# A two-layer decoder trunk: cross-attention's V projection moved to the start, half of K into layer 0's gated attention, layer 0's residual brought forward, FFN output parts of 8, 6 and 8 tiles

## The chip, the cores and the metric

The kernel runs on one core of one Trainium2 chip. The metric is the device time of one launch in microseconds (us). The kernel before was run three times: 1430.82, 1432.17 and 1435.38 us, median 1432.17. One further execution was profiled. All durations below come from that profile.

Engines are named as in the profile: PE is the matrix engine (PEld its weight loads), DVE the vector engine, ACT the activation engine, POOL the third elementwise engine, SP the engine that issues most DMA transfers. A name with q (SPq, PEq) is the engine's instruction queue.

## The reference

The input x is 512 tokens of 1024 numbers in fp32, `mem` is 256 memory tokens of 1024. After one layer norm come two layers, each of three sub-layers with `x <- LayerNorm(alpha*x + f(x))`:

```
proj = h @ w_in                          # columns: c_a 512, c_g 512, q 256, k 256, v 512, r 512, a_low 16
u  = silu(layer_norm(causal_conv31(c_a * sigmoid(c_g))))          # 31 taps per channel
o  = rms_norm(gla_chunked(q, k, v, log_a)) * silu(r)              # 4 heads, chunks of 64 tokens
h  = LN(alpha*h + concat(u, o) @ w_mix_out)
kv = mem @ w_xkv;  K, V = split(kv)                               # does not depend on h
h  = LN(alpha*h + softmax((h@w_xq) K^T / 16) V @ w_xo)            # 4 heads of 256
g, u = split(h @ w_ffn_in);  h = LN(alpha*h + (silu(g)*u) @ w_ffn_out)   # hidden width 2816
```

K and V of a layer need only `mem` and that layer's `w_xkv`, so they may be computed at any time before that layer's cross-attention.

## The kernel before, in words

Activations stay on chip, as four token tiles `h[0..3]` of 128 tokens by 1024. Every fp32 product is made of three matmuls in a reduced fp32 format (`mm3`, L136 to L139): high part by high part, high by low, low by high. So each operand, weight or activation, is split first (`split`, L100 to L102): ACT writes the high part (L101), DVE or POOL the difference (L102).

Weights come in chunks of 128 by 1024 numbers, 512 KB (`wchunk`, L121): a DMA on SP's queue into one of four `raw` buffers, then the split into one of four ring buffers `w`, or into a resident block. Which engine makes the low part goes in rotation over a list that `wlo_engines` sets; for layer 0's convolution, q/k, v and r weights it is POOL alone. `proj_feat` (L212) gives feature-major output, `proj_tok` (L237) token-major output, `out_proj` (L260) the products that end a sub-layer. `out_proj` goes token tile by token tile; each tile's two 512-column banks are added to h by DVE (L279), and where a norm follows, DVE computes statistics (L283) and the layer norm (L184 to L196) of that tile.

The order on each engine is set by a scheduler from priorities in the code; blocks under `tc.high_priority` go earlier, and the convolution taps (L600 and L602, 31 for each of four channel tiles, on DVE, accumulating in PSUM banks `cv`) have the lowest priority and fill DVE between other work.

The places in program order that the change touches:

1. **Front.** `mem` is loaded by two transfers and transposed (`mt`, L473, split into `mT`), then `mem_K` computes K of layer 0 in four head pairs `pr` (`xk`, weights `w_xk`), with the loads of x among their weight loads. Layer norm 0 runs on DVE and ACT meanwhile, its transposes are `lt_ln` (L533, evacuated at L535, split into `hT_ln`).
2. **Convolution input, gates, q and k.** `conv_in(0)` and `conv_in(1)` (`pp_c`, weights `w_c`) give u (L587), from which DVE's taps start. Then `gates()` and the q/k projection (`pp_qk`, evacuated at L659 to L663).
3. **Residual.** `residual0` (L540 to L546) puts layer norm 0's gain and bias onto h, on POOL, one multiplication and one addition of 128 by 1024 for each token tile; the gain and bias rows (`gb_ln`) are broadcast loads on SP's queue.
4. **Gated attention slot of layer 0.** `gla_pair(0)`, the r projection (`pt_r`), then V of layer 0 in two halves (`mem_V`, `pt_xv`, weights `w_xv`) as independent work for PE while the convolution's norm (`conv_norm`: transposes `cvt` L720, statistics and rsqrt on DVE, ACT L730, transposes back `cvb` L736, silu `csl` L738, split into `cUh`, `cUl`) and `gla_pair(1)` (`pa` L760, mask `attT` L765, `po` L775, norm L792 to L808, transposes `ogt`) go through DVE and ACT. Behind it comes the mixer's output projection `po_mo` with weights `w_mo`.
5. **FFN.** Hidden tiles of 128 are made in three parts (L905), and after each part `out_proj` (`po_fo`) adds the part's product into h. Layer 0's last part is followed by the next layer's `conv_in(0)`; layer 1's last part by the stores of the result.

Of the kernel before, what the change touches and what calls it, by code (L numbers as in the profile page):

```python
# [51 lines left out]
def trunk(ctx: ExitStack, tc, a, out):  # L52
# [47 lines left out]
    def split(hi, lo, src, eng=DVE):  # L100
        ACT.activation(hi, src, AF.Copy)  # L101
        eng.tensor_sub(lo, src, f(hi))  # L102
# [6 lines left out]
    def wlo_next():  # L109
        e = wlo[0][wlo[1] % len(wlo[0])]  # L110
        wlo[1] += 1
        return e
# [5 lines left out]
    def mov_hT(hT):  # L118
        return lambda kt: (hT[0][kt // 4][:, kt % 4, :], hT[1][kt // 4][:, kt % 4, :])

    def wchunk(src, nk, ncol, name, resident=False):  # L121

        raw = stage.tile([P, 1024], F32, tag="raw", name=f"raw_{name}")
        rv = raw.rearrange("p (k c) -> p k c", k=nk)
        nc.sync.dma_start(rv, src.rearrange("(k p) c -> p k c", p=P))
        if resident:
            w = block([P, 2, 1024], F32R, f"w_{name}")
        else:
            w = ring.tile([P, 2, 1024], F32R, tag="w", name=f"w_{name}")
        split(w[:, 0, :], w[:, 1, :], raw, wlo_next())  # L130
        return (
            w[:, 0, :].rearrange("p (k c) -> p k c", k=nk),
            w[:, 1, :].rearrange("p (k c) -> p k c", k=nk),
        )
# [99 lines left out]
                        for m, bk in enumerate(banks):  # L234
                            evac(m, bk[:, :n])

    def proj_tok(w, mov, c0, evac, name, groups=((0, 1), (2, 3))):  # L237


        wcs = [wchunk(w[ci * 2 * P:(ci + 1) * 2 * P, c0:c0 + 512], 2, 512, f"{name}{ci}") for ci in range(4)]  # L240
        for grp in groups:
            banks = {tt: bank(f"pt_{name}_{tt}") for tt in grp}
            for ci, (wh, wl) in enumerate(wcs):
                for tt in grp:
                    tsl = slice(tt * P, (tt + 1) * P)
                    for k in range(2):
                        kt = ci * 2 + k
                        mh, ml = mov(kt)
                        mm3(banks[tt], mh[:, tsl], ml[:, tsl], wh[:, k, :], wl[:, k, :],
                            kt == 0, kt == NK - 1)  # L250
            with tc.high_priority(offset=HP):
                for tt in grp:
                    evac(tt, banks[tt])
            yield
# [205 lines left out]
        return out  # L460


    def mem_T(name):
        mT = [block([P, NK, MEM], F32R, f"mT{j}_{name}") for j in range(2)]
        mraws = block([P, 2, D], F32, f"mem_{name}")
        for mt in range(2):
            nc.sync.dma_start(mraws[:, mt, :], a["mem"][0, mt * P:(mt + 1) * P, :])
        for mt in range(2):
            mraw = mraws[:, mt, :]
            for i in range(2):  # L470
                pt = bank(f"mt{mt}{i}_{name}", tag="tr")
                for k in range(4):
                    PE.transpose(pt[:, k * P:(k + 1) * P], mraw[:, (i * 4 + k) * P:(i * 4 + k + 1) * P], ident)  # L473
                ks, ms_ = slice(i * 4, i * 4 + 4), slice(mt * P, (mt + 1) * P)
                split(mT[0][:, ks, ms_], mT[1][:, ks, ms_], pt.rearrange("p (k t) -> p k t", k=4))
        return lambda kt: (mT[0][:, kt, :], mT[1][:, kt, :])
# [9 lines left out]
    def new_V(l):  # L486
        return [block([P, 2, D], F32R, f"V{j}_{l}") for j in range(2)]

    def mem_V(l, mT, V, c):
        cs = slice(c * 512, (c + 1) * 512)  # L490
        run(proj_tok(a["w_xkv"][l], mT, D + c * 512,
                     lambda mt, ps: split(V[0][:, mt, cs], V[1][:, mt, cs], ps), f"xv{c}_{l}", groups=((0, 1),)))


    def load_x(*tts):
        for tt in tts:
            nc.sync.dma_start(h[tt], a["x"][0, tt * P:(tt + 1) * P, :])

    lnrow = const.tile([2 * NK, P], F32, name="lnrow")
    nc.scalar.dma_start(lnrow[0:NK, :], a["ln0_g"].rearrange("(k p) -> k p", p=P))  # L500
    nc.scalar.dma_start(lnrow[NK:2 * NK, :], a["ln0_b"].rearrange("(k p) -> k p", p=P))
    mT = mem_T("0")
    pl = bank("lncol_ps", tag="tr")
    PE.transpose(pl[:, :2 * NK], lnrow, ident[:2 * NK, :2 * NK])
    lncol = const.tile([P, 2 * NK], F32, name="lncol")
    DVE.tensor_copy(lncol, pl[:, :2 * NK])
    KT = new_K(0)
    wlo_engines(DVE)
    mem_K(0, mT, KT, 0)
    wlo_engines(POOL, DVE)  # L510
    load_x(0, 1)
    mem_K(0, mT, KT, 1)
    load_x(2, 3)
    for pr in range(2, 4):
        mem_K(0, mT, KT, pr)
    hT = new_hT("ln0")
    with tc.high_priority(offset=HP):
# [33 lines left out]
    for l in range(L):  # L551
# [94 lines left out]
            DVE.tensor_copy(dec, qe[:, :, CH - 1::CH])  # L646

        conv_in(0)
        wlo_engines(POOL)
        if l > 0:  # L650
            mT = mem_T(f"{l}")
# [17 lines left out]
                PE.transpose(pt[:, tt * P:(tt + 1) * P], kd[:, hp, tt * P:(tt + 1) * P], ident)  # L669
            ACT.activation(kdT[:, hp].rearrange("p a b -> p (a b)"), pt, AF.Copy)  # L670
        v = block([P, NT, 512], F32, n_("v"))
        if l == 0:
            residual0(0, 1)
        run(proj_tok(w_in, mov, 1536, lambda tt, ps: ACT.activation(v[:, tt, :], ps, AF.Copy), n_("v")))


# [130 lines left out]
                ACT.activation(cOh[:, :, tsl], ptv, AF.Copy, scale=gnorm)  # L807
                DVE.scalar_tensor_tensor(cOl[:, :, tsl], ptv, gnorm, f(cOh[:, :, tsl]), ALU.mult, ALU.subtract)  # L808

        V = new_V(l)  # L810
        if l > 0:
            wlo_engines(DVE)
            mem_K(l, mT, KT, 0)
        gla_pair(0)
        run(proj_r)
        if l == 0:
            wlo_engines(POOL, DVE)
        for pr in range(1, 4) if l > 0 else ():
            mem_K(l, mT, KT, pr)
        for c in range(2):  # L820
            mem_V(l, mT, V, c)
        with tc.high_priority(offset=HP):
            conv_norm()
            gla_pair(1)
# [77 lines left out]


        w_fi, w_fo = a["w_ffn_in"][l], a["w_ffn_out"][l]
        for part, (j0, nj) in enumerate(((0, 8), (8, 8), (16, 6))):  # L905
            pT = []
            for j in range(j0, j0 + nj, 2):
                if (j - j0) % 4 == 0:
# [37 lines left out]
```

## Time and profile before

| what | value |
|---|---|
| three runs, median | 1432.17 us (1430.82 to 1435.38) |
| the profiled execution's own time | 1433.09 us |
| its span in the profile | 1431.4 us (1.7 us lie outside it) |
| PE busy | 1401.6 us (98%) |
| DVE busy | 1024.5 us (72%) |
| ACT busy | 608.2 us (42%) |
| POOL busy | 153.5 us (11%) |
| mean granted PE clock | 0.994 |

PE's idle time is 30 us in all; where it lies is the list of PE's waits. In a row of the timeline the first number is the start, the second the duration, then engine, line, operation, output<-input; a bracket gives the engine's idle time before it and what ended that. In a list of waits the numbers are the total, the count and the longest, in us. In a table of windows each engine has its busy time and, as (x), its instructions; PEclk is the granted clock, then come the DMA engines' busy share and GB/s.

### The profile page before, as it was taken

What the parts mean: (1) busy time and instruction counts of PE and PEld (TensorE: products, weight loads), DVE (VectorE), ACT (ScalarE), POOL (GpSimd) and SP (SyncE); (2) the same over time, 40 slices, a digit from 0 to 9 for tenths busy, and PEclk for the clock granted to TensorE, in tenths of its full rate; (3) what the DMA queues carried; (4) which work ended last, traced back from release to release, by engine and by line L of the source; (5) the groups of instructions that cost most, each with busy time, mean ns of one, the idle gap of its engine ahead of it and who ended that gap; (6) DMA issues with size and microseconds to landing.
All of it is one profiled execution on the core that took longest, in us unless ns stands there. A gap on an engine that the chain in (4) does not pass through costs nothing.

```text
span 1431.4 us, 22112 instructions
## 1 busy us (share of the span) xinstructions
PE 1401.6 (98%) x8943; PEld 1253.1 (88%) x8943; DVE 1024.5 (72%) x1700; ACT 608.2 (42%) x976; POOL 153.5 (11%) x98
## 2 busy tenths in 40 slices
PE   8999999999999999999999999999999999999997
PEld 7787878988999899899887889889889988998996
DVE  6699877666977376546769999775678764763767
ACT  5553361342456155335146235524524632560550
POOL 2266230000010000001013200000000000000000
PEclk9999999999999999999999999999999999999999
DMA  7423250321265265534342234412214652643641
GB/s 251 138 74 109 97 188 7 117 89 59 74 165 171 79 174 134 163 102 108 117 126 86 76 116 162 163 59 89 91 44 118 172 181 66 160 146 102 147 133 59
DMA packets 108730, 168.63 MB, mean 118 GB/s; under 512 B 7484, under 2 KB 81936, under 8 KB 108628
## 3 DMA queue, kind: packets, MB, share of 16 engines
q1 hardware_dynamic: 102548, 145.98, 31.6%
q0 software_dynamic: 5760, 20.97, 7.9%
q8 instruction: 70, 1.15, 0.3%
q14 instruction: 32, 0.26, 0.1%
q10 hardware_dynamic: 320, 0.27, 0.1%
HBM read 144.13 MB, written 2.10 MB: 102 GB/s over the span
## 4 chain that ended last, share of the span: by engine, by line
PE 87%; DVE 5%; DMA 3%; ACT 3%; issue 1%; POOL 0%; SPq 0%; DVEq 0%; POOLq 0%; ACTq 0%
PE po_fo L137 5%; PE po_fo L139 5%; PE po_fo L138 5%; PE fx L408 5%; PE fx L409 5%; PE fx L410 5%; PE fw L410 2%; PE fw L409 2%; PE fw L408 2%; PE pp_xq L137 2%; PE pp_xq L138 2%; PE pp_xq L139 2%; DMA s<-raw_a 2%; PE po_xo L138 2%; PE po_xo L139 2%; PE po_xo L137 2%
## 5 line engine op out<-in xcount | busy, mean ns | idle before, releaser
L602 DVE SCALAR_TENSOR_TENSOR cv<-u,chan,cv 128x511 f32<-128x511 f32 (+28 forms) x240 | 159.7, 730 | 0.3
L290 POOL DMA_DIRECT2D s<-raw_a x40 | 34.9, 885 | 981.8 <-PE pp_f L139 476.6
L138 PE MATMUL po_fo<-w_fo,ph 128*128 128x512 f32 (+1 forms) x358 | 138.1, 386 | 0.0
L139 PE MATMUL po_fo<-w_fo,pl 128*128 128x512 f32 (+1 forms) x358 | 137.1, 386 | 0.0
L137 PE MATMUL po_fo<-w_fo,ph 128*128 128x512 f32 (+1 forms) x358 | 131.9, 387 | 0.0
L101 ACT ACTIVATE w_a<-raw_a 128x1024 fp32r<-128x1024 f32 x60 | 63.3, 1054 | 148.9 <-PE po_fo L139 123.5
L102 DVE TENSOR_TENSOR w_s<-s,w_s 128x1024 fp32r<-128x1024 f32 x80 | 97.4, 1221 | 34.1 <-ACT w_s L101 33.6
L101 ACT ACTIVATE w_s<-s 128x1024 fp32r<-128x1024 f32 x80 | 83.8, 1052 | 47.5 <-DMA s<-raw_a 24.0
L408 PE MATMUL fx<-T_ln,w_s 128*128 128x256 f32 x320 | 91.0, 285 | 0.5 <-ACT u L421 0.2
L409 PE MATMUL fx<-T_ln,w_s 128*128 128x256 f32 x320 | 90.6, 283 | 0.0
L410 PE MATMUL fx<-T_ln,w_s 128*128 128x256 f32 x320 | 90.0, 283 | 0.0
L279 DVE SCALAR_TENSOR_TENSOR h<-h,po_fo 128x512 f32<-128x512 f32 (+1 forms) x49 | 32.3, 673 | 71.2 <-PE po_fo L139 71.2
L102 DVE TENSOR_TENSOR w_a<-raw_a,w_a 128x1024 fp32r<-128x1024 f32 x60 | 73.1, 1221 | 8.6 <-ACT w_a L101 7.4
L139 PEld LDWEIGHTS po_fo<-w_fo,pl 128*128 128x128 f32 x358 | 67.3, 188 | 13.3
L138 PEld LDWEIGHTS po_fo<-w_fo,ph 128*128 128x128 f32 x358 | 67.3, 188 | 13.1
L137 PEld LDWEIGHTS po_fo<-w_fo,ph 128*128 128x128 f32 x358 | 66.9, 188 | 12.8
L102 DVE TENSOR_TENSOR w_fo<-raw_fo,w_fo 128x1024 fp32r<-128x1024 f32 x44 | 53.0, 1221 | 14.8 <-ACT w_fo L101 14.7
L408 PEld LDWEIGHTS fx<-T_ln,w_s 128*128 128x128 f32 x320 | 61.5, 192 | 1.4 <-ACT u L421 0.7
L409 PEld LDWEIGHTS fx<-T_ln,w_s 128*128 128x128 f32 x320 | 61.5, 192 | 0.0
L138 PE MATMUL pp_xq<-hT_ln,w_xq 128*128 128x256 f32 (+1 forms) x192 | 61.3, 323 | 0.0
L410 PEld LDWEIGHTS fx<-T_ln,w_s 128*128 128x128 f32 x320 | 61.2, 192 | 0.0
L137 PE MATMUL pp_xq<-hT_ln,w_xq 128*128 128x256 f32 (+1 forms) x192 | 60.0, 321 | 0.5 <-ACT hT_ln L101 0.5
(317 smaller groups left out, 4420.6 us busy)
## 6 DMA issues: line engine op xcount, KB each, us to landing
raw_a<-w_ffn_in SPq DMA_DIRECT2D x60, 512.0 KB
raw_fo<-w_ffn_out SPq DMA_DIRECT2D x44, 512.0 KB
s<-raw_a POOLq DMA_DIRECT2D x40, 512.0 KB, 4.8
s<-w_ffn_in SPq DMA_DIRECT2D x20, 512.0 KB
raw_xk<-w_xkv SPq DMA_DIRECT2D x16, 512.0 KB
raw_c<-w_in SPq DMA_DIRECT2D x16, 512.0 KB
raw_xv<-w_xkv SPq DMA_DIRECT2D x16, 512.0 KB
raw_mo<-w_mix_out SPq DMA_DIRECT2D x16, 512.0 KB
```

The costliest lines, as they stand in the source:

```text
L101: ACT.activation(hi, src, AF.Copy)
L102: eng.tensor_sub(lo, src, f(hi))
L137: PE.matmul(o, lh, rh, start=start, stop=False)
L138: PE.matmul(o, lh, rl, start=False, stop=False)
L139: PE.matmul(o, ll, rh, start=False, stop=stop)
L279: DVE.scalar_tensor_tensor(h[tt][:, c0:c1], h[tt][:, c0:c1], scale, bks[c][:, :c1 - c0], ALU.mult, ALU.add)
L290: POOL.dma_start(dst, src, accum_op=ALU.add)
L408: PE.matmul(o, wh, bh, start=start and k == 0, stop=False, skip_group_check=True)
L409: PE.matmul(o, wh, bl, start=False, stop=False, skip_group_check=True)
L410: PE.matmul(o, wl, bh, start=False, stop=stop and k == 3, skip_group_check=True)
L602: DVE.scalar_tensor_tensor(cv[ct][:, s:], u[:, ct, :T - s], wj, cv[ct][:, s:], ALU.mult, ALU.add)
```

## The change

It has four parts. (a) `mem` is loaded by four quarter loads on ACT's queue; on SP's queue the V weights' first half comes first, then x, then V's second half, then the weights of K pairs 0 and 1. The first V weight chunk is split in two halves (`fine`). (b) In layer 0's gated attention slot stand K pairs 2 and 3 where both V halves stood, and `wlo_engines(DVE)` behind them gives all eight `w_mo` low parts to DVE (before, every second one was POOL's). (c) `residual0(0, 1)` is written directly behind `conv_in(0)`. (d) The FFN's parts are 8, 6 and 8 hidden tiles, not 8, 8 and 6.

```diff
--- before.py
+++ after.py
@@ -118,7 +118,7 @@
     def mov_hT(hT):
         return lambda kt: (hT[0][kt // 4][:, kt % 4, :], hT[1][kt // 4][:, kt % 4, :])
 
-    def wchunk(src, nk, ncol, name, resident=False):
+    def wchunk(src, nk, ncol, name, resident=False, fine=False):
 
         raw = stage.tile([P, 1024], F32, tag="raw", name=f"raw_{name}")
         rv = raw.rearrange("p (k c) -> p k c", k=nk)
@@ -127,7 +127,9 @@
             w = block([P, 2, 1024], F32R, f"w_{name}")
         else:
             w = ring.tile([P, 2, 1024], F32R, tag="w", name=f"w_{name}")
-        split(w[:, 0, :], w[:, 1, :], raw, wlo_next())
+        eng, step = wlo_next(), 512 if fine else 1024
+        for c0 in range(0, 1024, step):
+            split(w[:, 0, c0:c0 + step], w[:, 1, c0:c0 + step], raw[:, c0:c0 + step], eng)
         return (
             w[:, 0, :].rearrange("p (k c) -> p k c", k=nk),
             w[:, 1, :].rearrange("p (k c) -> p k c", k=nk),
@@ -234,10 +236,11 @@
                         for m, bk in enumerate(banks):
                             evac(m, bk[:, :n])
 
-    def proj_tok(w, mov, c0, evac, name, groups=((0, 1), (2, 3))):
-
-
-        wcs = [wchunk(w[ci * 2 * P:(ci + 1) * 2 * P, c0:c0 + 512], 2, 512, f"{name}{ci}") for ci in range(4)]
+    def proj_tok(w, mov, c0, evac, name, groups=((0, 1), (2, 3)), fine=False):
+
+
+        wcs = [wchunk(w[ci * 2 * P:(ci + 1) * 2 * P, c0:c0 + 512], 2, 512, f"{name}{ci}", fine=fine and ci == 0)
+               for ci in range(4)]
         for grp in groups:
             banks = {tt: bank(f"pt_{name}_{tt}") for tt in grp}
             for ci, (wh, wl) in enumerate(wcs):
@@ -460,11 +463,13 @@
         return out
 
 
-    def mem_T(name):
+    def mem_T(name, q=nc.sync, nq=1):
         mT = [block([P, NK, MEM], F32R, f"mT{j}_{name}") for j in range(2)]
         mraws = block([P, 2, D], F32, f"mem_{name}")
         for mt in range(2):
-            nc.sync.dma_start(mraws[:, mt, :], a["mem"][0, mt * P:(mt + 1) * P, :])
+            for c0 in range(0, D, D // nq):
+                cs = slice(c0, c0 + D // nq)
+                q.dma_start(mraws[:, mt, cs], a["mem"][0, mt * P:(mt + 1) * P, cs])
         for mt in range(2):
             mraw = mraws[:, mt, :]
             for i in range(2):
@@ -486,32 +491,33 @@
     def new_V(l):
         return [block([P, 2, D], F32R, f"V{j}_{l}") for j in range(2)]
 
-    def mem_V(l, mT, V, c):
+    def mem_V(l, mT, V, c, fine=False):
         cs = slice(c * 512, (c + 1) * 512)
         run(proj_tok(a["w_xkv"][l], mT, D + c * 512,
-                     lambda mt, ps: split(V[0][:, mt, cs], V[1][:, mt, cs], ps), f"xv{c}_{l}", groups=((0, 1),)))
+                     lambda mt, ps: split(V[0][:, mt, cs], V[1][:, mt, cs], ps), f"xv{c}_{l}", groups=((0, 1),), fine=fine))
 
 
     def load_x(*tts):
         for tt in tts:
             nc.sync.dma_start(h[tt], a["x"][0, tt * P:(tt + 1) * P, :])
 
+    mT = mem_T("0", q=nc.scalar, nq=2)
     lnrow = const.tile([2 * NK, P], F32, name="lnrow")
     nc.scalar.dma_start(lnrow[0:NK, :], a["ln0_g"].rearrange("(k p) -> k p", p=P))
     nc.scalar.dma_start(lnrow[NK:2 * NK, :], a["ln0_b"].rearrange("(k p) -> k p", p=P))
-    mT = mem_T("0")
+    V = new_V(0)
+    wlo_engines(DVE)
+    mem_V(0, mT, V, 0, fine=True)
+    load_x(0, 1)
+    wlo_engines(DVE, POOL)
+    mem_V(0, mT, V, 1)
+    load_x(2, 3)
     pl = bank("lncol_ps", tag="tr")
     PE.transpose(pl[:, :2 * NK], lnrow, ident[:2 * NK, :2 * NK])
     lncol = const.tile([P, 2 * NK], F32, name="lncol")
     DVE.tensor_copy(lncol, pl[:, :2 * NK])
     KT = new_K(0)
-    wlo_engines(DVE)
-    mem_K(0, mT, KT, 0)
-    wlo_engines(POOL, DVE)
-    load_x(0, 1)
-    mem_K(0, mT, KT, 1)
-    load_x(2, 3)
-    for pr in range(2, 4):
+    for pr in range(2):
         mem_K(0, mT, KT, pr)
     hT = new_hT("ln0")
     with tc.high_priority(offset=HP):
@@ -646,6 +652,8 @@
             DVE.tensor_copy(dec, qe[:, :, CH - 1::CH])
 
         conv_in(0)
+        if l == 0:
+            residual0(0, 1)
         wlo_engines(POOL)
         if l > 0:
             mT = mem_T(f"{l}")
@@ -669,8 +677,6 @@
                 PE.transpose(pt[:, tt * P:(tt + 1) * P], kd[:, hp, tt * P:(tt + 1) * P], ident)
             ACT.activation(kdT[:, hp].rearrange("p a b -> p (a b)"), pt, AF.Copy)
         v = block([P, NT, 512], F32, n_("v"))
-        if l == 0:
-            residual0(0, 1)
         run(proj_tok(w_in, mov, 1536, lambda tt, ps: ACT.activation(v[:, tt, :], ps, AF.Copy), n_("v")))
 
 
@@ -807,18 +813,19 @@
                 ACT.activation(cOh[:, :, tsl], ptv, AF.Copy, scale=gnorm)
                 DVE.scalar_tensor_tensor(cOl[:, :, tsl], ptv, gnorm, f(cOh[:, :, tsl]), ALU.mult, ALU.subtract)
 
-        V = new_V(l)
         if l > 0:
+            V = new_V(l)
             wlo_engines(DVE)
             mem_K(l, mT, KT, 0)
         gla_pair(0)
         run(proj_r)
         if l == 0:
             wlo_engines(POOL, DVE)
-        for pr in range(1, 4) if l > 0 else ():
+        for pr in range(1 if l > 0 else 2, 4):
             mem_K(l, mT, KT, pr)
-        for c in range(2):
+        for c in range(2) if l > 0 else ():
             mem_V(l, mT, V, c)
+        wlo_engines(DVE)
         with tc.high_priority(offset=HP):
             conv_norm()
             gla_pair(1)
@@ -902,7 +909,7 @@
 
 
         w_fi, w_fo = a["w_ffn_in"][l], a["w_ffn_out"][l]
-        for part, (j0, nj) in enumerate(((0, 8), (8, 8), (16, 6))):
+        for part, (j0, nj) in enumerate(((0, 8), (8, 6), (14, 8))):
             pT = []
             for j in range(j0, j0 + nj, 2):
                 if (j - j0) % 4 == 0:
```

All lines behind the edits move down by 2 to 7. The order of instructions at three places follows.

PE at the front, before (`w_xk_000` is the first chunk of K's weights, `mT_0` the split transposed memory):

```order
L473 MATMUL mt_0_112<-ident,mem_109 128x128 x4
L473 MATMUL mt_0_119<-ident,mem_109 128x128 x4
L473 MATMUL mt_0_126<-ident,mem_109 128x128 x4
L473 MATMUL mt_0_133<-ident,mem_109 128x128 x4
L137 MATMUL pp_xk_000_156<-mT_0_107,w_xk_000_148 128x256
L137 MATMUL pp_xk_001_157<-mT_0_107,w_xk_000_148 128x256
L504 MATMUL lncol_ps<-ident,lnrow 128x16
L138 MATMUL pp_xk_000_156<-mT_0_108,w_xk_000_148 128x256
L139 MATMUL pp_xk_000_156<-mT_0_107,w_xk_000_148 128x256
L137 MATMUL pp_xk_000_156<-mT_0_107,w_xk_000_148 128x256
```

PE at the front, after (`pt_xv_0_0` is the V bank of the first 128 memory tokens, `w_xv_00` to `w_xv_03` the four weight chunks):

```order
L478 MATMUL mt_0_111<-ident,mem_106 128x128 x4
L478 MATMUL mt_0_118<-ident,mem_106 128x128 x4
L139 MATMUL pt_xv_0_0_166<-w_xv_00_146,mT_0_104 128x512
L140 MATMUL pt_xv_0_0_166<-w_xv_00_146,mT_0_104 128x512
L141 MATMUL pt_xv_0_0_166<-w_xv_00_146,mT_0_105 128x512
L139 MATMUL pt_xv_0_0_166<-w_xv_00_146,mT_0_104 128x512
L140 MATMUL pt_xv_0_0_166<-w_xv_00_146,mT_0_104 128x512
L141 MATMUL pt_xv_0_0_166<-w_xv_00_146,mT_0_105 128x512
L139 MATMUL pt_xv_0_0_166<-w_xv_01_153,mT_0_104 128x512
L478 MATMUL mt_0_125<-ident,mem_106 128x128 x4
L140 MATMUL pt_xv_0_0_166<-w_xv_01_153,mT_0_104 128x512
L141 MATMUL pt_xv_0_0_166<-w_xv_01_153,mT_0_105 128x512
```

V's first matmuls follow the transposes of the first 128 memory tokens; the first transposes of the other 128 stand behind seven of them, the rest later, and `lncol_ps` later still.

On POOL, all four multiplications of the residual and two of its additions now stand ahead of low parts of the two `w_c` chunks (`w_c_010`, `w_c_011`) that `conv_in(1)` needs last; before, they stood behind the first two `w_qk` chunks. On SP's queue the residual's two row loads stand behind the first `w_qk` load.

PE in the gated attention slot of layer 0, the last rows ahead of the mixer's output projection's start, before:

```order
L139 MATMUL pt_xv_0_1_1651<-w_xv_03_1647,mT_0_108 128x512
L137 MATMUL pt_xv_0_1_1651<-w_xv_03_1647,mT_0_107 128x512
L138 MATMUL pt_xv_0_1_1651<-w_xv_03_1647,mT_0_107 128x512
L139 MATMUL pt_xv_0_1_1651<-w_xv_03_1647,mT_0_108 128x512
L775 MATMUL po_0_1834<-v_1154,attT_579 128x128 x4
L775 MATMUL po_0_1835<-v_1154,attT_579 128x128 x4
L785 MATMUL po_0_1834<-S_1290,qk_581 64x128
L736 MATMUL cvb_0_1776<-ident,acc_0_577 128x128 x4
L785 MATMUL po_0_1834<-S_1290,qk_581 64x128
L785 MATMUL po_0_1835<-S_1290,qk_581 64x128
L736 MATMUL cvb_0_1785<-ident,acc_0_577 128x128 x4
```

and after:

```order
L140 MATMUL pp_xk_001_1655<-mT_0_105,w_xk_001_1651 128x256
L141 MATMUL pp_xk_001_1655<-mT_0_104,w_xk_001_1651 128x256
L811 MATMUL ogt_0_1509<-ident,og_0_1504 128x128 x4
L811 MATMUL ogt_0_1521<-ident,og_0_1516 128x128 x4
L726 MATMUL cvt_0_1747<-ident,acc_0_603 128x128 x2
L726 MATMUL cvt_0_1747<-ident,acc_0_604 128x128 x2
L766 MATMUL pa_0_1816<-qk_607 64x64 x8
L726 MATMUL cvt_0_1755<-ident,acc_0_603 128x128 x2
L726 MATMUL cvt_0_1755<-ident,acc_0_604 128x128 x2
L766 MATMUL pa_0_1817<-qk_607 64x64 x8
L781 MATMUL po_0_1838<-v_1187,attT_605 128x128 x4
L791 MATMUL po_0_1838<-S_1316,qk_607 64x128 x8
```

Before, 18 V matmuls stand between the last `pa` and the first `po`; after, the last K matmul stands ahead of `ogt`, `cvt`, `pa` and `po`, with no other work among them.

DVE at the end of layer 1, from the add of the last token tile's last bank on (`h_102` is token tile 2, `h_103` tile 3), before:

```order
L279 SCALAR_TENSOR_TENSOR h_103<-h_103,po_fo_1_3_2_13458 128x256
L154 TENSOR_SCALAR t_ln_12_13444<-y_ln_12_13443,v_ln_12_13439 128x1
L283 BN_STATS st_fo_13_13513<-h_103 128x6
L160 TENSOR_SCALAR s_ln_12_13445<-t_ln_12_13444 128x1
L184 BN_AGGR mv_ln_13_13521<-st_fo_13_13513 128x2
L160 TENSOR_SCALAR y_ln_12_13443<-s_ln_12_13445,y_ln_12_13443 128x1
L186 TENSOR_SCALAR v_ln_13_13523<-mv_ln_13_13521 128x1
L190 SCALAR_TENSOR_TENSOR h_103<-h_103,mv_ln_13_13521,gb_ln_1_13237 128x512 x2
L196 SCALAR_TENSOR_TENSOR h_102<-h_102,y_ln_12_13443,gb_ln_1_13237 128x512 x2
```

and after, from the add of that tile's first bank on:

```order
L282 SCALAR_TENSOR_TENSOR h_103<-h_103,po_fo_1_3_0_13448 128x512
L198 SCALAR_TENSOR_TENSOR h_102<-h_102,y_ln_12_13435,gb_ln_1_13183 128x512 x2
L286 BN_STATS st_fo_13_13523<-h_103 128x6 x2
L282 SCALAR_TENSOR_TENSOR h_103<-h_103,po_fo_1_3_1_13449 128x256
L286 BN_STATS st_fo_13_13523<-h_103 128x6
L282 SCALAR_TENSOR_TENSOR h_103<-h_103,po_fo_1_3_2_13450 128x256
L286 BN_STATS st_fo_13_13523<-h_103 128x6
L186 BN_AGGR mv_ln_13_13531<-st_fo_13_13523 128x2
L188 TENSOR_SCALAR v_ln_13_13533<-mv_ln_13_13531 128x1
```

The pair of L196 for `h_102` stood behind the last tile's L190, and stands now (as L198) behind the add of the last tile's first bank.

## The prediction

> **What bounds the kernel now.** I read the page's head first, then PE's waits, then windows around the longest of them, then the timelines of PE, DVE and POOL there.
>
> ```profile
> span 1431.4 us, 22112 instructions
> PE 1401.6 (98%) x8943; PEld 1253.1 (88%) x8943; DVE 1024.5 (72%) x1700; ACT 608.2 (42%) x976; POOL 153.5 (11%) x98
> ```
>
> PE is busy for 98% of the span. The change adds and removes no matrix work, so it can gain only out of PE's 30 us of idle time and out of stretches at a reduced clock. PE's list of waits (total, count, longest) says where these are:
>
> ```profile
> PE mt L473 <- DMA mem<-mem: 4.4, 1, 4.4
> PE pt_v L137 <- DVE qk L659: 2.0, 1, 2.0
> PE lt_ln L533 <- ACT xf L535: 1.8, 1, 1.8
> PE pp_c L137 <- DVE h L279: 1.5, 1, 1.5
> PE pp_xk L137 <- ACT mT L101: 1.2, 1, 1.2
> PE po L775 <- DVE attT L765: 1.1, 1, 1.1
> PE po_mo L137 <- ACT cUh L101: 0.9, 1, 0.9
> PE lncol_ps L504 <- DVE mT L102: 0.9, 1, 0.9
> PE mt L473 <- DVE mT L102: 0.6, 1, 0.6
> ```
>
> Four rows (mt twice, pp_xk, lncol_ps) are the first 12 us; lt_ln is the end of layer norm 0; pt_v is the wait for q's evacuation; po and po_mo lie in layer 0's gated attention slot; pp_c is the boundary between the layers. The windows show that some waits cost more than their length:
>
> ```profile
> 12.00:14.00 2.00, 2.00 (x11) 2.00 (x11) 2.00 (x4) 0.17 (x1) 0.00 (x0) 0.50 1.11 368
> 118.00:120.00 2.00, 2.00 (x6) 1.52 (x6) 2.00 (x4) 0.05 (x1) 2.00 (x2) 0.50 0.79 258
> 726.00:728.00 2.00, 2.00 (x12) 2.00 (x11) 1.94 (x8) 0.42 (x1) 0.00 (x0) 0.50 0.80 244
> 700.00:720.00 20.00, 20.00 (x94) 16.59 (x93) 19.42 (x46) 4.04 (x5) 0.00 (x0) 1.00 0.00 1
> ```
>
> Behind the front's waits, the pt_v wait and the boundary's waits the granted clock (third number from the right) stands at 0.50 for some 3.4 us with its flanks, so each costs about 1.7 us more. The last row shows DVE at 19.42 of 20 us ahead of the boundary: there DVE, not PE, is the tight engine.
>
> The page "TensorE: Matmul & The Clock Gate" of the Trainium skill (section "What's actually happening") has the clock halved only after an idle window of about 3.4 us. By that rule the 2.0 us wait would cost no clock, removing the boundary's wait would be worth 1.9 us instead of 3.6, and the sum below would come to 1430 instead of 1428. The 0.50 of the window from 118 us, right behind that wait, speaks against it, and the measurement decides.
>
> **What is moved.** Pitch of back-to-back matmuls, from rows 32 and 31 steps apart:
>
> ```profile
> 175.21 0.39 PE L137 MATMUL pt_xv<-w_xv,mT 128*128 128x512 f32 x1
> 182.46 0.40 PE L139 MATMUL pt_xv<-w_xv,mT 128*128 128x512 f32 x1
> 20.29 0.28 PE L137 MATMUL pp_xk<-mT,w_xk 128*128 128x256 f32 x1
> 24.01 0.28 PE L138 MATMUL pp_xk<-mT,w_xk 128*128 128x256 f32 x1
> ```
>
> That is 0.227 us for a V matmul and 0.12 us for a K one. V has 2 halves x 8 x 2 x 3 = 96 matmuls, 21.75 us; two K pairs have as many, 11.5 us. So 10.25 us of PE work leave the gated attention slot and go to the front. In a sum that balances; what counts is the waiting at each place.
>
> **Front, -2.5 us (0 to -5).** Before, the rows above give 4.4 + 0.6 + 1.2 + 0.9 = 7.1 us of waits, 1.7 us of clock and 1.8 us for lt_ln: 10.6 us lost.
>
> ```profile
> GB/s 0 0 75 287 398 362 342 298 347 366 376 399 405 429 380 372 360 351 351 396 394 421 375 370 353 353 345 345 339 304 313 236 79 0 0 0 12 0 124 347
> 1.75 1.28 ACT L101 ACT_TABLE_LOAD   x1 [1.75 <-PEq L936]
> 8.26 1.06 ACT L101 ACTIVATE w_xk<-raw_xk 128x1024 fp32r<-128x1024 f32 x1 [1.25 <-DMA raw_xk<-w_xkv]
> 9.35 1.23 DVE L102 TENSOR_TENSOR w_xk<-raw_xk,w_xk 128x1024 fp32r<-128x1024 f32 x1 [1.61 <-ACT w_xk L101]
> ```
>
> The first row has 0.7 us slices of the first 28 us: the queue moves about 365 GB/s from 2 us on, whichever queue issued. mem and V's first half are 3.15 MB, landed at 2 + 8.6 = 10.6 us; a chunk's split adds 1.06 + 1.23, six matmuls 1.36, and V's second token half 24 x 0.227 = 5.4: V's first half is done at about 19.7 us. x's 2.1 MB come next, so V's second half has its first chunk at 17.8 + 2.3 = 20.1 us. By then PE has done 10.9 us of V and 1.9 us of transposes: 7.3 us lost. Layer norm 0's chain then lies under V's second half and K, so lt_ln no longer waits. That gives -3.3. I take -2.5, because the table load and the fourfold issue now stand ahead of ACT's splits. If chunks never held PE, 5.6 us would be lost (-5); if every row of before recurs in other places, 0. The split of mem's load moves no byte sooner at this rate and counts 0; splitting the first chunk brings its first half some 1.1 us forward, within the range.
>
> **Residual on POOL and the conv/qk stretch, -1 us (0 to -3.6).**
>
> ```profile
> 61.43 2.40 POOL L102 TENSOR_TENSOR w_c<-raw_c,w_c 128x1024 fp32r<-128x1024 f32 x1 [1.53 <-ACT w_c L101]
> 79.43 0.39 PE L137 MATMUL pp_c<-hT_ln,w_c 128*128 128x512 f32 x1
> 89.00 11.40 POOL L545 TENSOR_TENSOR h<-h,gb_ln 128x1024 f32<-128x1024 f32 x4
> 91.31 2.10 DVE L643 TENSOR_TENSOR dk<-dk 128x1024 f32<-128x1024 f32 x1
> 782.62 1.21 DVE L643 TENSOR_TENSOR dk<-dk 128x1024 f32<-128x1024 f32 x1
> ```
>
> The four multiplications (11.4 us) move ahead of `w_c_010`'s low part, which was made from 61.43 to 63.83 and whose chunk PE first uses at 79.43 (by its place in PE's order): after, it is ready at about 61.4 + 11.4 + 2.4 = 75, 4.4 us early. The move frees DVE: L643 took 2.10 us beside the residual and 1.21 us in layer 1 with POOL idle. L639 has the same kind of excess; together I count 1 us, since q/k's low parts now stand there on POOL. "SBUF — State Buffer" (section "SBUF: two separate sides") says that a DVE operation with two SBUF inputs and a POOL operation exclude each other; the two L643 rows agree.
>
> The pt_v wait gets shorter too, but what PE gains there it waits for a little later: the gated attention slot starts when DVE's taps are done, and their number is unchanged. If that were not so, 2.0 + 1.7 us would come on top; hence the far end.
>
> **Gated attention slot, +4.5 us (+2.4 to +12).** Here the removed matmuls were cover.
>
> ```profile
> 163.72 3.63 DVE L602 SCALAR_TENSOR_TENSOR cv<-u,chan,cv 128x482 f32<-128x482 f32 x5
> 180.02 2.78 DVE L102 TENSOR_TENSOR w_xv<-raw_xv,w_xv 128x1024 fp32r<-128x1024 f32 x1
> 182.71 0.15 DVE L726 SCALAR_TENSOR_TENSOR b<-mv,y_cln 128x2 f32<-128x2 f32 x1
> 193.82 1.46 DVE L158 SCALAR_TENSOR_TENSOR y_cln<-t_cln,y_cln 128x2 f32<-128x2 f32 x1
> 197.01 0.16 DVE L726 SCALAR_TENSOR_TENSOR b<-mv,y_cln 128x2 f32<-128x2 f32 x1
> 202.97 0.50 PE L137 MATMUL po_mo<-w_mo,cUh 128*128 128x512 f32 x1
> 209.64 0.50 PE L137 MATMUL po_mo<-w_mo,cUh 128*128 128x512 f32 x1 [0.92 <-ACT cUh L101]
> ```
>
> The chain is: taps end (167.35), statistics and rsqrt of two token tiles, first L726 at 182.71, the other two tiles, second L726 at 197.01, transposes back, silu, `cUh`, `po_mo`. The first L726 stays (182.5): a `w_mo` part takes the place of the `w_xv` one before it, which took 2.78 us where 1.23 is usual, and gains little. From there to the second were 14.3 us, in which DVE also made a `w_xv` low part (1.23), V's low parts (1.3) and a 1.46 us step that takes 0.16 elsewhere, and `cvt` and `pa` stood behind V matmuls on PE; without those, and with two more `w_mo` low parts on DVE, I get about 8.9: second L726 at 191.4, `po_mo` at 195.1, its third weight step at 204.1 instead of 209.64. So PE arrives 7.9 and then 5.5 us earlier, where its work shrank by 10.25: it waits 2.4 to 4.7 us longer, and such waits can cost clock. I take 4.5. Far end: nothing of the 10.25 is gained, with 1.7 us of clock.
>
> **FFN parts, -3.5 us at the boundary (0 to -3.6), -1.5 us at the end (0 to -1.8).**
>
> ```profile
> 719.07 2.35 DVE L102 TENSOR_TENSOR w_c<-raw_c,w_c 128x1024 fp32r<-128x1024 f32 x2
> 722.66 0.68 DVE L279 SCALAR_TENSOR_TENSOR h<-h,po_fo 128x512 f32<-128x512 f32 x1
> 1422.82 1.40 DVE L190 SCALAR_TENSOR_TENSOR h<-h,mv_ln,gb_ln 128x512 f32<-128x512 f32 x2
> 1424.14 1.41 DVE L196 SCALAR_TENSOR_TENSOR h<-h,y_ln,gb_ln 128x512 f32<-128x512 f32 x2
> 1427.01 1.67 DVE L196 SCALAR_TENSOR_TENSOR h<-h,y_ln,gb_ln 128x256 f32<-128x256 f32 x4
> ```
>
> With 8 instead of 6 hidden tiles PE takes 48 x 0.227 = 10.9 us for a token tile, not 8.2; DVE's work on a tile is about 8.5 us (two adds of 0.68, two statistics as long, L190 1.40, L196 1.41, two splits of about 0.7 and some 1.6 of small steps, an estimate). DVE no longer falls behind, the add at 722.66 (late behind 3.6 us of `w_c` splits) comes in time, and 1.9 us of waits with 1.7 us of clock go. At the end, token tile 2's pair at 1424.14 stood between the last tile's L190 and its rsqrt; it moves ahead of the last matmul. The middle part's 6 tiles have no norm behind them and cost nothing.
>
> **Sum.** -2.5 - 1 + 4.5 - 3.5 - 1.5 = -4.0 against the profiled execution's 1433.09 (span 1431.4 and 1.7 outside): 1429.1. That execution is 0.9 above the median of the runs, so **1428.2**.
>
> **Rivals** (about 4.3 us, 0.3%, is what can be told from no change):
> - Nothing is regained in the slot: DVE's taps and norm chain set `po_mo`'s start, +12 in place of +4.5, so 1435.7, slower. It decides from 8.5 us of new waiting on. Against it: V's low parts and the blocked steps do leave that chain.
> - The front gains all: -5, slot +2.4: 1423.6. For it, the 365 GB/s; against it, ACT's issues and table load ahead of the splits.
> - The front gains nothing and the boundary half, since the first split waits as long for its chunk as before: 1432.5.
> - The residual's rows land late and hold `w_c_010` past its 4.4 us of slack: 8 us late would be 3.6 us of PE waiting and 1.7 of clock: 1433.5. Against it: its loads follow one 512 KB load.
>
> **Chances.** My forecast 0.42 (own range 1426 to 1430.5), the second rival 0.20, the third 0.20, the first 0.11, the fourth 0.07. Below 1427.9 lie the second and half of my own: 0.40. Above 1436.5 lies part of the first and of mishaps: 0.09. The range 1423 to 1435 leaves out the first rival and a little on each side.
>
> **What would show it.** PE's first V matmul near 7.5 us and no lt_ln wait; the residual's L551 ahead of `w_c_010` with no pp_c wait; 3 to 8 us of PE waits for cvt, pa, po, cvb or po_mo in layer 0; no wait for h L282 and full clock at the boundary; L198 of tile 2 ahead of the last add. I am wrong if the slot's waits exceed 8 us, or the front still loses 10.

## The result and the profile after

The changed kernel takes 1444.49 us (median of 6 runs, 1440.25 to 1446.08) against 1431.72 us before: the ratio is 1.0079, 95% interval 1.0060 to 1.0097. It is 0.8% slower, where 1428.2 (1423 to 1435) was forecast. The execution profiled is the fastest of the six, 1440.25 us, with a mean granted clock of 0.996; the other five have 0.988 to 0.994 and no profile. The head of its page and PE's waits:

```profile
span 1438.5 us, 22130 instructions
PE 1401.8 (97%) x8949; PEld 1253.3 (87%) x8949; DVE 1024.6 (71%) x1706; ACT 607.8 (42%) x977; POOL 140.5 (10%) x93
```

```profile
PE mt L478 <- DMA mem<-mem: 7.5, 2, 6.6
PE po_fo L139 <- DVE h L282: 6.8, 2, 3.8
PE po_mo L139 <- ACT cUh L101: 2.4, 1, 2.4
PE cvt L726 <- ACT acc L736: 2.1, 1, 2.1
PE cvt L726 <- ACT acc L610: 1.8, 1, 1.8
```

PE's work is the same 1401.8 us; the waits are others. The second row is new, and no step of the prediction has it: twice, once in each layer, PE waits for DVE's add into h. The place is the FFN's middle part, now 6 hidden tiles. DVE and POOL there in layer 0, after the change, from two timelines (the bracket is idle time and what ended it):

```profile
574.81 0.87 POOL L293 DMA_DIRECT2D s<-raw_a  x1 [27.00 <-DVE pl L102]
```

```profile
573.75 0.69 DVE L102 TENSOR_TENSOR pl<-sg,ph 128x512 fp32r<-128x512 f32 x1
582.91 1.23 DVE L395 TENSOR_TENSOR s<-s,raw_a 128x1024 f32<-128x1024 f32 x1 [8.47 <-DMA s<-raw_a]
584.05 2.48 DVE L282 SCALAR_TENSOR_TENSOR h<-h,po_fo 128x512 f32<-128x512 f32 x4
```

and before, at the same place of the program:

```profile
594.08 0.86 POOL L290 DMA_DIRECT2D s<-raw_a  x1 [29.15 <-DMA raw_a<-w_ffn_in]
```

```profile
601.01 1.22 DVE L392 TENSOR_TENSOR s<-s,raw_a 128x1024 f32<-128x1024 f32 x1 [7.92 <-DMA s<-raw_a]
602.16 1.28 DVE L279 SCALAR_TENSOR_TENSOR h<-h,po_fo 128x512 f32<-128x512 f32 x2
```

L395 is an addition in `swiglu_seven` for the next part's first weights (`s2 = s1 + r11`); it needs `s1`, into which POOL's queue adds `r22` by an accumulating transfer (`add_into`). In DVE's order it stands ahead of the adds into h. So DVE is idle for 8 us, in both kernels, until the transfer lands, 7 to 8 us after its issue (the median of the 40 such transfers is 4.7). Before, with 8 hidden tiles, PE needs 10.9 us for a token tile, 21.8 us for two, and asks for token tile 0's banks again at about 604 (six of these 96 matmuls came early, the others run from 583.78 on): they were freed at 603. After, with 6 hidden tiles, two token tiles are 16.3 us; PE asks at 581.8, and the adds begin at 584:

```profile
584.78 0.50 PE L139 MATMUL po_fo<-w_fo,ph 128*128 128x512 f32 x1 [2.99 <-DVE h L282]
```

All four bank adds then come in one run, and PE has lost 3.0 us; the granted clock stays at 1.00 behind this wait. In layer 1 the wait is 3.8 us, and the clock is halved behind it:

```profile
1286.00:1288.00 2.00, 0.86 (x2) 0.77 (x3) 2.00 (x4) 0.00 (x0) 0.00 (x0) 0.69 0.00 0
1288.00:1290.00 2.00, 2.00 (x6) 1.52 (x6) 0.88 (x2) 0.00 (x0) 0.00 (x0) 0.50 0.00 0
```

The boundary between the layers went as forecast: the wait of `pp_c` for h is gone from the list. In the window from 720 to 740 us, first of before, then of after, PE is now busy throughout and at full clock:

```profile
720.00:740.00 20.00, 17.82 (x130) 16.68 (x129) 15.72 (x34) 5.05 (x9) 0.00 (x0) 0.91 0.40 113
```

```profile
720.00:740.00 20.00, 20.00 (x141) 18.75 (x140) 16.15 (x32) 5.72 (x8) 0.00 (x0) 1.00 0.43 114
```

At the end, tile 2's norm now precedes the last add, and from that add to the end of the span it is 8.8 us, where it was 9.9 before (1421.48 to 1431.4):

```profile
1424.53 1.41 DVE L198 SCALAR_TENSOR_TENSOR h<-h,y_ln,gb_ln 128x512 f32<-128x512 f32 x2
...
1429.67 0.42 DVE L282 SCALAR_TENSOR_TENSOR h<-h,po_fo 128x256 f32<-128x256 f32 x1 [1.99 <-PE po_fo L141]
```

### The profile page after: what moved, and what is told of

It is laid out like the page before. It is cut to its first block, busy times and chain, and to the rows that moved or that the text cites. A ratio compares the mean times of both kernels' runs of the same rounds, so it can differ in the third digit from the quotient of the medians.

```text
span 1438.5 us, 22130 instructions
## 1 busy us (share of the span) xinstructions
PE 1401.8 (97%) x8949; PEld 1253.3 (87%) x8949; DVE 1024.6 (71%) x1706; ACT 607.8 (42%) x977; POOL 140.5 (10%) x93
## 4 chain that ended last, share of the span: by engine, by line
PE 83%; DVE 9%; DMA 4%; ACT 3%; issue 1%; POOL 0%; ACTq 0%; DVEq 0%; POOLq 0%
PE po_fo L139 5%; PE po_fo L141 5%; PE po_fo L140 5%; PE fx L411 5%; PE fx L413 5%; PE fx L412 5%; DVE cv L608 4%; DMA s<-raw_a 3%; PE fw L413 2%; PE fw L412 2%; PE fw L411 2%; PE pp_xq L139 2%; PE pp_xq L140 2%; PE pp_xq L141 2%; PE po_mo L139 2%; PE po_xo L141 2%
## 5 line engine op out<-in xcount | busy, mean ns | idle before, releaser
L608 DVE SCALAR_TENSOR_TENSOR cv<-u,chan,cv 128x511 f32<-128x511 f32 (+29 forms) x240 | 159.7, 732 | 0.2
L101 ACT ACTIVATE w_a<-raw_a 128x1024 fp32r<-128x1024 f32 x60 | 63.2, 1054 | 145.5 <-PE po_fo L141 119.9
L101 ACT ACTIVATE w_s<-s 128x1024 fp32r<-128x1024 f32 x80 | 83.8, 1052 | 46.9 <-DMA s<-raw_a 29.8
```

What stands on the lines that cost most here:

```text
L608: DVE.scalar_tensor_tensor(cv[ct][:, s:], u[:, ct, :T - s], wj, cv[ct][:, s:], ALU.mult, ALU.add)
```

## Experiments

Three rounds each, 10 runs (4 for `slot_k4`), beside runs of before on the same chip (medians 1432.1 to 1432.5). In the texts put down ahead of each run, theory A puts the loss on the middle part and DVE's queue, B and C on the moved work; S puts what is left on the slot (too little cover for the chain there), F on the front.

**1. The parts alone, on the kernel before.**

```diff
-        for part, (j0, nj) in enumerate(((0, 8), (8, 8), (16, 6))):
+        for part, (j0, nj) in enumerate(((0, 8), (8, 6), (14, 8))):
```

> The kernel before with nothing but the FFN parts 8, 6, 8. Theory A (in the middle part, DVE's queue stands at the addition L392, which waits for POOL's accumulating transfer, ahead of the adds into h that free PE's banks; two token tiles of 6 hidden tiles are over before the transfer lands): PE waits 3 to 4 us for DVE's add into h in the middle part of each layer, in part with a halved clock behind it, 8 us together; the layer boundary gains 3.6 and the end 1.1; 1434 to 1437 us. Rival B (the middle part's loss comes from the moved front and slot, not from the part's size): no such wait, 1427 us.

1437.15 us, ratio 1.0026 (1.0008 to 1.0044). PE's first row of waits:

```profile
PE po_fo L137 <- DVE h L279: 6.0, 2, 3.0
```

Two waits of 3.0 us, and the granted clock drops to 0.5 behind both. A holds; the parts by themselves cost 4.7 us.

**2. The same, with the addition of each part's first group on POOL.** It moves one addition, and with it the wait for the transfer, from DVE's queue to POOL's, where the addition takes 2.39 us for 1.22.

```diff
-    def swiglu_seven(w, q, j, ph, pl, i0, name):
+    def swiglu_seven(w, q, j, ph, pl, i0, name, first=False):
...
-        DVE.tensor_add(s2, s1, r11)
+        (POOL if first else DVE).tensor_add(s2, s1, r11)
...
-                    pT += swiglu_seven(w_fi, quads, j, ph, pl, (j - j0) % 4, f"{l}")
+                    pT += swiglu_seven(w_fi, quads, j, ph, pl, (j - j0) % 4, f"{l}", first=j == j0)
```

> As the run with parts 8, 6, 8, with the one addition L392 of each part's first group on POOL in place of DVE, so that DVE's queue no longer waits for the transfer. Theory A: no wait for the adds into h; boundary and end keep their gain; 1426 to 1428 us. Rival B or a rival by which DVE is simply too busy there: the waits stay, or POOL's slower addition (2.4 us for 1.2) makes the next group late: 1431 or more.

1427.82 us, ratio 0.9963 (0.9946 to 0.9979): 9.3 us less than run 1 and 4.6 less than before. POOL now does the waiting, and DVE's add comes as soon as PE is done with a bank:

```profile
579.88 2.39 POOL L392 TENSOR_TENSOR s<-s,raw_a 128x1024 f32<-128x1024 f32 x1 [6.29 <-DMA s<-raw_a]
```

```profile
576.97 1.28 DVE L279 SCALAR_TENSOR_TENSOR h<-h,po_fo 128x512 f32<-128x512 f32 x2 [5.13 <-PE po_fo L139]
```

The two waits for h are gone from PE's list. They were 6.0 us, and PE's busy time, which a halved clock lengthens, falls by 2.8 us (1403.8 to 1401.0); together that is the difference of the two spans, 8.8 us (1437.1 to 1428.3). So A is shown, and this is the version that beats both kernels. The edit moves the addition in every part, not only in the middle one; the addition on POOL with the parts of before was not run.

**3. The changed kernel with the parts of before.**

```diff
-        for part, (j0, nj) in enumerate(((0, 8), (8, 6), (14, 8))):
+        for part, (j0, nj) in enumerate(((0, 8), (8, 8), (16, 6))):
```

> The changed kernel with the parts of before (8, 8, 6). Theory A: the middle part's waits go (8 us and what clock they cost), the boundary's wait of 1.9 us with 1.7 of clock comes back, the end gets 1.1 longer: 3 to 7 us faster than the changed kernel, 1438 to 1441 us, and what is left above before, 6 to 9 us, is the gated attention slot. Rival C (the slot and the front carry all of the loss): 1444 us or more.

1439.62 us, ratio 1.0046 (1.0030 to 1.0063): 4.9 us less than the changed kernel. The wait for h in the middle part is gone, the boundary's wait of 1.5 us (`pp_c` for h) is back.

**4. The changed kernel with the POOL addition** (the edit of run 2).

> The changed kernel with the addition of each part's first group on POOL. Theory A: no PE wait for the adds into h, 8 to 12 us less than the changed kernel, 1433 to 1436 us. Rival C: 1444 us. If it lands below before's 1431.7, the moved front and slot together cost nothing.

1434.15 us, ratio 1.0009 (0.9995 to 1.0023): 10.3 us less than the changed kernel, so the wait in the middle parts was that much of it. Against run 2, which has the same FFN, the moved front, slot and residual cost 6.3 us. Its trace differs from the changed kernel's in the slot of layer 0, with the same order of instructions there. Window 192 to 208, first the changed kernel, then this one:

```profile
192.00:208.00 16.00, 12.54 (x116) 9.49 (x116) 10.71 (x25) 10.14 (x20) 0.00 (x0) 1.00 0.44 150
```

```profile
192.00:208.00 16.00, 15.79 (x101) 13.09 (x102) 7.23 (x22) 5.87 (x15) 0.00 (x0) 0.50 0.35 128
```

With the clock at 0.50 for all 16 us PE does 101 instructions for 116, and it is busy for 15.79 of them. `cUh` (ACT L101), which `po_mo` needs, follows the second L732 in both, but first ends late here:

```profile
198.32 0.16 DVE L732 SCALAR_TENSOR_TENSOR b<-mv,y_cln 128x2 f32<-128x2 f32 x1
...
201.47 0.63 ACT L101 ACTIVATE cUh<-csl 128x512 fp32r<-128x512 f32 x1
```

```profile
199.22 0.16 DVE L732 SCALAR_TENSOR_TENSOR b<-mv,y_cln 128x2 f32<-128x2 f32 x1
...
206.17 0.63 ACT L101 ACTIVATE cUh<-csl 128x512 fp32r<-128x512 f32 x1
```

3.2 us in the first, 7.0 us in the second: on PE the products `po` and the transposes `cvb` stand between them, at half rate (14 matmuls of `po` take 1.97 us for 1.08). The profiles of runs 3 and 4 and of run 8 below all have that half clock, from 192 to 196 on until about 208; the changed kernel's own profile, its fastest run, has not. The waits do not tell the two apart: ahead of 192 both traces have a wait of 1.8 us and one of 2.1 us (`cvt`), and from there until `po_mo` runs PE waits for nothing in the half-clock trace. What keeps the clock at half is not shown.

The price of it is less than the 5.3 us by which `po_mo` starts later: at the end of `po_mo` this execution is 3.1 us behind the changed kernel's (256.6 for 253.5), which has its own half clock from 208 to 212. And of run 4's ten executions the two with a mean granted clock of 0.996 (1433.07 and 1433.39 us) are only some 1.5 us below the median of the other eight (0.992 and 0.993).

**5 to 7. Other divisions of V and K between front and slot,** all with the POOL addition. K pairs 1 to 3 in the slot:

```diff
-    for pr in range(2):
+    for pr in range(1):
         mem_K(0, mT, KT, pr)
...
-        for pr in range(1 if l > 0 else 2, 4):
+        for pr in range(1, 4):
```

> The changed kernel with the POOL addition, and with K pairs 1, 2, 3 (17.2 us of matmuls) in layer 0's gated attention slot, pair 0 alone at the front. Theory S (in the slot DVE's and ACT's norm chain sets the end, some 9 us later than PE's work there, and the waits keep the clock halved): the front ends 5.75 us earlier and the slot's end moves with it: 1426 to 1429 us, against 1434.2. Rival F (what was lost is the moved front itself, not the cover): 1434 us.

1431.59 us, ratio 0.9995 (0.9978 to 1.0012). 2.6 us less than run 4, not the 5 to 8 expected. The runs spread from 1428.2 to 1435.8; the profile, of one of its faster runs (1428.65), has the clock halved in the slot only around 172 and from 202 to 206. The mean granted clock does not explain the spread: the three runs below 1429 have 0.995, and so has the slowest; the other six, 1430.4 to 1433.4, have 0.996.

V's second half in the slot beside two K pairs:

```diff
-    mem_V(0, mT, V, 1)
...
-        for c in range(2) if l > 0 else ():
+        for c in range(2) if l > 0 else (1,):
             mem_V(l, mT, V, c)
```

> The changed kernel with the POOL addition, and with V's second half beside K pairs 2 and 3 in the slot (22.4 us of matmuls, before had 21.75); the front keeps V's first half and K pairs 0 and 1. Theory S: the slot loses nothing against before, the front and the convolution stretch keep their gain of 2 to 6 us: 1422 to 1426 us. Rival F: 1430 us or more.

1433.40 us, ratio 1.0003 (0.9990 to 1.0015). With as much cover as before it is not faster, against S, but the run does not test the cover alone. Without V's second half ahead of it, layer norm 0 makes PE wait again (`lt_ln`, 2.6 us) and the clock halves behind it, so the gate projection (`al`) begins at 67.2 us where before had 64.3. And an addition of the gates on DVE takes 8.54 us for 1.23 beside POOL's operations, an effect that run 11 below shows by itself; the taps, which DVE makes behind it, end at 174.7 us, where run 5, whose gates began 0.5 us later, had 171.8:

```profile
89.17 8.54 DVE L642 TENSOR_TENSOR qk<-qk 128x1024 f32<-128x1024 f32 x1 [3.95 <-ACT qk L641]
```

All four K pairs in the slot:

```diff
-    for pr in range(2):
-        mem_K(0, mT, KT, pr)
...
-        for pr in range(1 if l > 0 else 2, 4):
+        for pr in range(1 if l > 0 else 0, 4):
```

> The changed kernel with the POOL addition, and with all four K pairs (23 us) in the slot; the front has V alone. Theory S: as with V's second half there, 1422 to 1427 us, if layer norm 0, which then has only V as cover at the front, does not make PE wait; with such a wait 2 us more. Rival F: 1432 us or more.

1443.58 us, ratio 1.0080 (1.0060 to 1.0100). Far from S's 1422 to 1427, or 2 us more with a wait of `lt_ln`. That wait is 2.9 us, `pp_qk` and `pt_v` wait 1.9 to 2.0 us for weights, and `po_mo` starts at 220 us (before 203). The same addition takes 12.12 us here, and the taps end at 176.2 us although the gate projection starts at 64.8, 2.9 us ahead of run 5's:

```profile
83.67 12.12 DVE L641 TENSOR_TENSOR qk<-qk 128x1024 f32<-128x1024 f32 x1 [2.50 <-ACT qk L640]
```

So the amount of cover alone does not decide, and runs 6 and 7 do not settle S: they also shift the gates against the residual on POOL. How much of run 7's 9.4 us above run 4 is that, and why 23 us of K do worse in the slot than 21.75 of V, stays open.

**8. The residual at its old place,** with the POOL addition.

```diff
         conv_in(0)
-        if l == 0:
-            residual0(0, 1)
...
         v = block([P, NT, 512], F32, n_("v"))
+        if l == 0:
+            residual0(0, 1)
```

> The changed kernel with the POOL addition, and the residual's first half written where before had it, behind q and k. Theory S says that PE's gain before the slot (4.6 us in the trace of the changed kernel) is lost again to waits in the slot, and that DVE's taps gain 1 to 2 us from the earlier residual: 1434 to 1437 us against 1434.2, with the 2 us wait for q's evacuation back. Rival R (the earlier residual itself delays the low parts that PE needs): faster than 1433.

1434.00 us, ratio 1.0014 (1.0004 to 1.0024), the same as run 4. In run 4 the v projection ends at 144.1 us, here at 148.6, with the old wait for q's evacuation (1.9 us) and its half clock. But `po_mo` starts at 207.5 there and at 207.0 here: what PE gains before the slot it gives back in it.

**9. Work that nothing reads, in the slot** (48 matmuls of 256 columns on `mT`, 5.75 us, output not used), on run 4.

```diff
+        if l == 0:
+            fb = bank("fill")
+            for x in range(48):
+                mh = mT(x % NK)[0]
+                PE.matmul(fb[:, :256], mh[:, :P], mh, start=True, stop=True)
         wlo_engines(DVE)
         with tc.high_priority(offset=HP):
             conv_norm()
```

> The changed kernel with the POOL addition, and 48 more matmuls of 256 columns (5.75 us of PE work on operands that are at hand, into a bank that nothing reads) in layer 0's slot, where its order has them between the last K matmul, ogt, cvt and pa. Theory H (in the slot PE mostly waits, and the waits halve the clock from 192 to 208 us, which costs 4 to 5 us): the extra work is free or better than free, 1429 to 1434 us against 1434.2, with full clock from 192 to 208. Rival W (PE's time is full there, the half clock costs nothing): 1439 to 1440 us.

1433.01 us, ratio 1.0002 (0.9992 to 1.0012): with 5.75 us more work it is no slower than run 4 (1.1 us faster, with intervals that overlap). All ten executions have a mean granted clock of 0.997 or more, where eight of run 4's ten had 0.992 or 0.993. The same window:

```profile
192.00:208.00 16.00, 14.16 (x157) 12.86 (x156) 8.99 (x25) 8.71 (x22) 0.00 (x0) 1.00 0.40 135
```

Full clock, 157 instructions for 101. So PE's waits in the slot were longer than 5.75 us with the clock they cost.

**10. mem's loads on SP's queue,** ahead of the V weights, on run 4.

```diff
-    mT = mem_T("0", q=nc.scalar, nq=2)
+    mT = mem_T("0", nq=2)
```

> The changed kernel with the POOL addition, and the four quarter loads of mem on SP's queue ahead of the V weights, not on ACT's. If the loads of the two queues share the engines, so that mem's first half lands late (PE's first transpose at 6.6 us for 4.4 before), the first transpose comes at 4 to 4.6 us and layer 0's gate projection 1 to 2 us earlier: 1432 to 1433.5 us against 1434.2. Rival: the V weights, then behind mem, come as much later as mem comes earlier; 1434.2 or more.

1432.69 us, ratio 1.0004 (0.9990 to 1.0018), 1.5 us less than run 4, whose runs it overlaps. PE's first transposes, here and in the changed kernel:

```profile
3.87 1.94 PE L478 MATMUL mt<-ident,mem 128*128 128x128 f32 x8 [3.87 <-DMA mem<-mem]
```

```profile
6.65 1.09 PE L478 MATMUL mt<-ident,mem 128*128 128x128 f32 x4 [6.65 <-DMA mem<-mem]
```

Loads on two queues share the DMA engines: with V's weights beside it PE's first transpose, which waits for mem, comes 2.8 us later, and the gate projection starts 2.0 us later (72.7 in run 4 for 70.7). V gained nothing by it: its first matmul is at 9.86 us in the changed kernel and at 9.20 here.

**11. The residual's move alone,** on run 2.

```diff
         conv_in(0)
+        if l == 0:
+            residual0(0, 1)
...
         v = block([P, NT, 512], F32, n_("v"))
-        if l == 0:
-            residual0(0, 1)
```

> The kernel before with parts 8, 6, 8 and the POOL addition (1427.8 us), and with the residual's first half behind conv_in(0). By the run with the residual at its old place, the earlier residual frees PE of 4 us before the slot and the slot takes them back: 1426.5 to 1429 us. Rival: with 21.75 us of V as cover in the slot the gain stays: 1423 to 1425 us.

1435.30 us, ratio 1.0019 (1.0008 to 1.0029): 7.5 us slower than run 2. Neither expectation had this. Run 2's and this run's gates, L637 (an addition of two SBUF tiles on DVE), and POOL beside it here:

```profile
84.92 1.23 DVE L637 TENSOR_TENSOR qk<-qk 128x1024 f32<-128x1024 f32 x1 [2.50 <-ACT qk L636]
```

```profile
75.93 9.50 POOL L546 TENSOR_TENSOR h<-h,gb_ln 128x1024 f32<-128x1024 f32 x4
85.35 7.14 POOL L102 TENSOR_TENSOR w_qk<-raw_qk,w_qk 128x1024 fp32r<-128x1024 f32 x3
```

```profile
83.53 10.04 DVE L637 TENSOR_TENSOR qk<-qk 128x1024 f32<-128x1024 f32 x1 [2.49 <-ACT qk L636]
```

L637 takes 10.04 us for 1.23: it starts within the last of the four additions and ends at 93.57, 1.1 us behind the end of POOL's unbroken run of additions and low parts. The long additions of runs 6 and 7 end 1.1 us behind such a run too. All of DVE's queue stands behind it, the taps too, which end at 172.5 us for 168.6. In the changed kernel the same addition meets POOL at another phase and takes 2.38 us.

**12. Run 5 with mem's loads on SP's queue** (the edits of runs 5 and 10 together).

> The changed kernel with the POOL addition, K pairs 1 to 3 in the slot (1431.6 us) and mem's quarter loads on SP's queue. If both gains add: 1429 to 1431 us, with the slot's waits as in the run with three pairs; if the clock in the slot is halved in some executions only, they spread from 1427 to 1435 us as there.

1430.19 us, ratio 0.9985 (0.9969 to 1.0002): about the two gains together, and not below run 2.

## Why the prediction was wrong

By its own steps, with what the traces show:

- **FFN parts.** The step that failed is one sentence: "The middle part's 6 tiles have no norm behind them and cost nothing." I priced DVE's work there and not what DVE's queue waits for. In its place the runs show PE waiting there in both layers (3.0 and 3.8 us) for adds that stand behind a DMA wait in DVE's queue. These waits, with the clock behind them, cost 9.3 us (runs 1 and 2) to 10.3 us (run 4 and the changed kernel). The idle time was in the trace of before (7.92 us ahead of L392), and harmless only while a pair of token tiles took PE 21.8 us, with about 1 us to spare. The two terms beside it held: boundary and end gave -4.6 in run 2, for -3.5 and -1.5.
- **Front, -2.5.** The gate projection starts at 72.4, where before's 64.3 and 10.25 of moved work give 74.55: -2.1. That lt_ln no longer waits is right; V's first matmul came at 9.86 us, for 7.5. "The split of mem's load moves no byte sooner ... and counts 0" was wrong: on ACT's queue it brought mem 2.8 us later, and cost 2.0 at the gate projection (run 10; 1.5 in the medians, whose intervals overlap). The 365 GB/s "whichever queue issued" did not hold at the start: from 2 to 6 us it was 225 GB/s in the changed kernel, 287 in run 10 and 334 before.
- **Residual, -1.** Its worth in the changed kernel is nothing (run 8), as the reason given (the slot takes it back) has it. The 1 us for a freer DVE was wrong in sign: the four DVE operations of the gates took 2.42, 6.03, 1.21 and 0.16 us (run 4), 9.8 in all, for 1.23, 4.49, 2.10 and 1.08, 8.9, at the old place (run 8). That a DVE operation with two SBUF inputs and a POOL operation exclude each other was cited from the Trainium skill ("SBUF — State Buffer", section "SBUF: two separate sides"); run 11 agrees and shows how far it goes, 10.04 us.
- **Slot, +4.5.** In the changed kernel's profile the second L732 is at 198.3, where the forecast's 191.4, moved by its own 10.25 - 2.5 - 1, has 198.2, and `po_mo` starts at 202.2 for 201.9; PE's waits for `cvt`, `ogt`, `po`, `cvb` and `po_mo` there are 7.5 us, where 3 to 8 were forecast. That the times hit so closely is in part luck: the taps ended at 176.3, 2.2 us later than forecast, and the steps from there to the second L732 took 2.0 us less. At the end of `po_mo` that execution stands 2.2 us behind before; front, residual and slot together were forecast at +1.0. What was mis-sized is the clock: I allowed 1.7 us, at the far end alone, and in the profiles of runs 3, 4 and 8 it stays at half for 12 to 16 us, so that `po_mo` starts about 5 us later (207.5) and, in run 4, ends 3.1 us later. That the other five runs of the changed kernel, 3 to 6 us above the profiled one, had this too is inferred and not shown: their mean granted clock is lower (0.988 to 0.994 for 0.996), but they have no profile, and in run 4 a lower clock goes with only 1.5 us.

The sum of medians is then: 10.3 us for the middle parts (9.3 on the kernel before), 6.3 for front, residual and slot (forecast +1.0), -4.6 for boundary and end: +12.0, where +12.8 was measured. The first rival, the slowest of the four, had the slot alone as its cause, and would have given 1435.7. No rival had the middle parts.

On the clock, the page "TensorE: Matmul & The Clock Gate" of the Trainium skill (section "What's actually happening") has it halved after an idle window of about 3.4 us. Run 4 has it halved with no wait on the list above 2.1 us in the slot, and before had it behind a single wait of 1.96 us. But longer waits passed without it: 2.99 us in the middle part of the changed kernel's layer 0. So the length of a wait does not decide alone, and what does, these runs do not show.

## What to carry to other kernels

An engine's queue is a list: before a stage is shortened, look on each engine that frees its buffers for an instruction that waits for a transfer ahead of the ones that free them, and compare that wait with the time the shorter stage leaves. A long idle time of an engine off the path is not free cover but a deadline: here 8 us of idle DVE were harmless at 21.8 us of PE work and cost 3 to 4 us at 16.3, in part with a half clock behind. When matmuls are taken from a stage in which PE covers a chain of small steps, count the clock as well as the waits.

## What was not expected of the hardware

- A DVE operation with two SBUF inputs can wait through several POOL operations, not one: 10.04 us for 1.23 in run 11, 8.54 in run 6 and 12.12 in run 7, each ending 1.1 us behind POOL's unbroken run.
- The clock can stay at 0.50 while PE is busy: 15.79 of 16 us in run 4, on short matmuls and transposes that the changed kernel's profile has at 1.00. With 5.75 us of useless matmuls ahead of them it was 1.00 (run 9).
- The length of a wait does not say whether the clock halves behind it: 1.96 us halved it (before, 118 us), 2.04 us in run 7 (104 us) and 2.99 us in the changed kernel (585 us) did not, and 3.0 us did, in both layers of run 1.
- Loads issued on two queues at once slow each other: PE's first transpose of mem comes at 6.65 us beside V's weights, at 3.87 ahead of them (run 10), and from 2 to 6 us all loads together moved 225 GB/s for 287.
